# One 512-column product in place of two in the output and down-projections of a two-layer trunk

## The chip, the cores and the metric

One core of a Trainium2 chip runs the whole program in one launch. The metric is the device time of one execution in microseconds (us), the median of several executions. TensorE (PE in the profile) multiplies; VectorE (DVE) and ScalarE (ACT) do the elementwise work; the DMAs are issued from SyncE's queue (SP). All weights and activations lie in HBM as fp32.

## What is computed

The reference is a decoder trunk of two layers over 256 tokens of width 1024, cut here to what matters:

```python
for i in range(DEPTH):                      # 2 layers
    mod = sc @ w_ada[i] + b_ada[i]          # six rows of 1024: shift, scale, gate, twice
    sh_m, sc_m, g_m, sh_f, sc_f, g_f = jnp.split(mod, 6, axis=-1)
    h = modulate(x, norm_mix[i], sh_m, sc_m)
    y = moba_attention(h, ..., w_o[j], ...) if i % 2 == 0 else short_conv(h, ..., w_out[j])
    x = x + g_m[:, None, :] * y
    h = modulate(x, norm_ffn[i], sh_f, sc_f)
    x = x + g_f[:, None, :] * swiglu(h, w_gate_up[i], w_down[i])   # hidden width 2816
```

Attention has 8 heads of width 128, the convolution has width 3. The change is in the three kinds of products that end a sub-layer: `@ w_o` (attention's output), `@ w_out` (the convolution's output) and `@ w_down`, each followed by the gated addition to x.

## The kernel before

**Layout.** x is kept transposed in SBUF as `xT`: 8 column tiles (k = 0 to 7) of 128 features by 256 tokens. Activations that enter a product have the same layout. Weights are the stationary operand, 128 by 128; the 256 tokens stream past them.

**Precision.** Every fp32 operand is split in a high and a low part (fp32r): ACT makes the high part, DVE subtracts it for the low part. A product of two fp32 operands is three products, `mm3` (L246): high weights with the high activations (L248), high weights with the low activations (L249), low weights with the high activations (L250), summed in PSUM. Names ending in h and l are the parts: `wh_o`, `wl_o` for the weights, `ovh`, `ovl` for attention's output, `zvh`, `zvl` for the convolution's, `a0h`, `a0l` (layer 0) and `a1h`, `a1l` (layer 1) for the hidden activations of the channel mixer.

**Weights.** They come in pieces of 1 MB (256 output columns by 8 row tiles; the last piece of a down-projection has 6): a DMA (L88) into one of 5 buffers `wf`, then `prep` (L91) makes `wh` on ACT (L98) and `wl` on DVE (L99), each in two halves of 4 row tiles, into one of 3 buffers each. `get` (L240) prepares up to two pieces ahead. Between them pieces of `w_ada` come by the same five buffers (`wa`) and are summed on DVE into the shifts, scales and gates (`prod`, L109).

**The projections.** `out_proj` (L360) makes the 1024 output features as 4 column pairs j of two tiles o each. `op_o` and `op_co` have 8 row tiles to sum, `op_d` has 22. For `op_o` and `op_co` the pairs run in the groups [0, 1], [2], [3], for `op_d` each alone. Each (j, o) has a PSUM tile of one bank (4 in turn). After a group, at high priority, `residual` (L357) adds the gated sum to `xT` on DVE, one instruction of 128x256 for each (j, o), and `Norm.take` (L312) begins the next norm: squares on ACT (`sq_n`), their sum on DVE (`ss_n`), and the unnormalized next input in two parts (`a0h` on ACT, `a0l` on DVE; `zvh`, `zvl` before the convolution).

**The next sub-layer's start.** `raw_gemm` (L398) multiplies that unnormalized input for the first pieces before the norm is known (`raw_f`, `raw_m`: 96 products of 258 columns, the two extra columns carrying the shift). While it runs, the mean square goes over PE (`ms_n`), ACT (`sd_n`), DVE (`rs_n`), PE (`rr_n`) and ACT (`rrow_n`), and DVE and ACT make the normalized input (`t_f`, `f0h`, `f0l`; `m1h`, `m1l`) for the rest.

**Order.** A scheduler orders each engine's instructions from the program's order, its priorities and its own estimate of when things are ready. So instructions of `op_o` and of `raw_f` may stand between each other.

The stages in the profile: `op_o` until 130.4 us (its first group between attention's heads from 98 us), `raw_f` until 143.1, gate and up of layer 0 until 254, `op_d` of layer 0 until 318.4, `raw_m` until 331, the convolution's input until 388, `op_co` until 411, `raw_f` of layer 1 until 423.7, its gate and up until 533, its `op_d` until 592.7.

Of the kernel before, what the change touches and what calls it, by code (L numbers as in the profile page):

```python
# [8 lines left out]
F32 = mybir.dt.float32  # L9
# [6 lines left out]
P = 128  # L16
S = 256
# [16 lines left out]
def trunk_kernel(ctx: ExitStack, tc: tile.TileContext, x_t, cols_in, scale_in, shift_in, ada_in, qk_rows, kv_in, o_in,  # L34
# [106 lines left out]


    def room(tag, n, name, dtype=F32):
        size = {"al": KF * S + 16, "ah": KF * S, "zh": KD * (S + 32), "zl": KD * (S + 2)}.get(tag, KD * S)
        return act.tile([P, size], dtype, tag=tag, name=name)[:, 16 if tag == "al" else 0:][:, :n]

# [5 lines left out]

    room("al", 1, "first_al")
    xT = act.tile([P, KD, S], F32, name="xT")
    hs = new_pair("h", "m0", KD)
    room("ah", 1, "first_ah")
    x_tok = room("zh", 2 * D, "x_tok").rearrange("p (t d) -> p t d", d=D)
    for t in range(2):
# [87 lines left out]
    def mm3(ps, lhs, rhs, first, last):  # L246
        (ah, al), (bh, bl) = lhs, rhs
        nc.tensor.matmul(ps, ah, bh, start=first, stop=False, skip_group_check=True)  # L248
        nc.tensor.matmul(ps, ah, bl, start=False, stop=False, skip_group_check=True)  # L249
        nc.tensor.matmul(ps, al, bh, start=False, stop=last, skip_group_check=True)  # L250

    def feat_gemm(parts, xs, nk):
# [21 lines left out]

    RAW = KD * (S + 2)

    def wide_pair(name):
        flat = [room("z" + p, RAW, name + p, F32R) for p in "hl"]
        return (tuple(f[:, :KD * S].rearrange("p (k s) -> p k s", s=S) for f in flat),
                tuple(f.rearrange("p (k s) -> p k s", s=S + 2) for f in flat))  # L280

    def raw_in(pair):
        flat = [t.rearrange("p k s -> p (k s)") for t in pair]
        return tuple(f[:, KF * S - RAW:].rearrange("p (k s) -> p k s", s=S + 2) for f in flat)

# [71 lines left out]
    def residual(ps, l, gate, k):  # L357
        nc.vector.scalar_tensor_tensor(xT[:, k], ps, mcol(l, gate, k), xT[:, k], op0=ALU.mult, op1=ALU.add)

    def out_proj(keys, xs, l, gate, done, between={}):  # L360
        groups = [[0, 1], [2], [3]] if len(keys[0]) == 1 else [[j] for j in range(4)]
        for js in groups:
            pss = {(j, o): psum.tile([P, S], F32, tag="gemm", name=f"op_{keys[j][0][0][0]}_{l}_{j}_{o}", bufs=4)
                   for j in js for o in range(2)}
            base = 0
            total = sum(nk for _, nk in keys[0])
            for i, (_, nk) in enumerate(keys[0]):
                ws = {j: get(keys[j][i][0]) for j in js}
                tiles = [(j, o, k) for j in js for o in range(2) for k in range(nk)]
                if js[0] == 0:  # L370
# [12 lines left out]
            with tc.high_priority(400):  # L383
                for (j, o), ps in pss.items():
                    residual(ps, l, gate, 2 * j + o)
                    done(2 * j + o)

    def split(dst, k, src, name, psum_src=False):
        nc.scalar.activation(dst[0][:, k], src, AF.Copy)
        nc.vector.tensor_sub(dst[1][:, k], src, dst[0][:, k].bitcast(F32))  # L390
# [36 lines left out]
    def ffn(l, norm, av, done):  # L427
        for j in range(KF // 2):
# [6 lines left out]
            else:  # L435
# [102 lines left out]
    with tc.manual_schedule(engines={mybir.EngineType.PE, mybir.EngineType.DVE, mybir.EngineType.Activation}):  # L538
# [212 lines left out]

    av = new_pair("a", "a0", KF)
    n0 = Norm("n0", 0, SH_F, SC_F, raw_in(av))
    out_proj([[(("o", j), KD)] for j in range(4)], ov, 0, G_M, n0.take, between(6))
    zv, zraw = wide_pair("zv")
    n1 = Norm("n1", 1, SH_M, SC_M, zraw)
# [110 lines left out]
```

## Time and profile before

| | |
|---|---|
| time, median of 3 runs | 597.29 us (597.12 to 597.96) |
| the profiled execution's own time | 597.81 us |
| its span in the trace | 596.0 us |
| granted TensorE clock | 1.00 |
| DMA, share of the 16 engines' span | 69.9%, 156.04 MB |

Times within the trace count from the span's start. In rows of the trace the columns are: start, busy time, engine, line, operation, output <- inputs, shapes, count of merged records, and in square brackets the idle time before it with what ended it. A record of a product lasts longer than the spacing of the products' starts, since they are pipelined; costs are read from the spacing. A plain fp32 product (not fp32r) is recorded as two passes. PEld is PE's loading of the 128x128 weights, which overlaps the products.

### The profile page before, as it was taken

The page shows a single profiled execution, that of the slowest core. Times are in us where ns is not written, and L with a number is a line of the kernel's source. Part 1 is how long each engine was busy: PE and PEld are TensorE (multiplying, and loading weights), DVE is VectorE, ACT ScalarE, POOL GpSimd, SP SyncE. Part 2 cuts the span into 40 slices and gives each one's busy share as a digit, 9 for nine tenths or more (in the row PEclk, how much of TensorE's full clock was granted, in tenths as well). Part 3 has the DMA queues.
Part 4 walks back from the last instruction along what each step waited for, and adds up shares of the span by engine and source line. Part 5 has one row for each costly group of instructions (what it writes and reads, how often), then busy time and mean ns, then how long its engine had stood idle before and what let it go on. Part 6 is the DMA issues. An engine that isn't in the chain of part 4 may idle for free.

```text
span 596.0 us, 12024 instructions
## 1 busy us (share of the span) xinstructions
PE 587.8 (99%) x5036; PEld 579.0 (97%) x5036; DVE 454.5 (76%) x719; ACT 314.1 (53%) x526; POOL 1.1 (0%) x8
## 2 busy tenths in 40 slices
PE   7999999999999999999999999999999999999997
PEld 6899999999999999999999999999999999999997
DVE  4789898898988879877877998659987566564440
ACT  6457799596544544534444754437844554443330
POOL 0000000000000000000000000000000000000000
PEclk9999999999999999999999999999999999999999
DMA  8999988945897899777987477544486574655400
GB/s 323 392 373 411 361 332 300 369 162 180 329 388 296 303 358 356 268 279 276 330 317 292 148 293 278 207 142 184 170 323 249 206 283 164 252 186 190 165 19 18
DMA packets 25109, 156.04 MB, mean 262 GB/s; under 512 B 2784, under 2 KB 3168, under 8 KB 8928
## 3 DMA queue, kind: packets, MB, share of 16 engines
q1 hardware_dynamic: 25056, 155.28, 69.9%
q8 instruction: 39, 0.64, 0.4%
q14 instruction: 14, 0.11, 0.1%
HBM read 154.22 MB, written 1.05 MB: 261 GB/s over the span
## 4 chain that ended last, share of the span: by engine, by line
PE 89%; DVE 4%; DMA 3%; ACT 2%; issue 1%; SPq 0%; DVEq 0%; ACTq 0%
PE pu L250 7%; PE pu L249 7%; PE pu L248 7%; PE op_d L249 7%; PE op_d L248 7%; PE op_d L250 7%; PE pg L249 6%; PE pg L248 6%; PE pg L250 6%; PE op_o L248 1%; PE raw_f L248 1%; PE raw_f L249 1%; PE op_o L250 1%; PE op_co L250 1%; PE raw_f L250 1%; DMA wa<-in_ada_dram 1%
## 5 line engine op out<-in xcount | busy, mean ns | idle before, releaser
L109 DVE SCALAR_TENSOR_TENSOR prod<-wa,c_all 128x1024 f32<-128x1024 f32 x80 | 97.6, 1220 | 13.9 <-DMA wa<-in_ada_dram 13.0
L98 ACT ACTIVATE wh_d<-wf_d 128x1024 fp32r<-128x1024 f32 (+1 forms) x48 | 45.3, 981 | 67.2 <-issue 46.5
L99 DVE TENSOR_TENSOR wl_d<-wf_d,wh_d 128x1024 fp32r<-128x1024 f32 (+1 forms) x48 | 52.9, 1132 | 26.4 <-ACT wh_d L98 26.4
L98 ACT ACTIVATE wh_g<-wf_g 128x1024 fp32r<-128x1024 f32 x44 | 45.7, 1051 | 47.0 <-issue 47.0
L98 ACT ACTIVATE wh_u<-wf_u 128x1024 fp32r<-128x1024 f32 x44 | 44.5, 1051 | 48.4 <-issue 48.0
L99 DVE TENSOR_TENSOR wl_u<-wf_u,wh_u 128x1024 fp32r<-128x1024 f32 x44 | 52.2, 1219 | 16.7 <-ACT wh_u L98 16.5
L99 DVE TENSOR_TENSOR wl_g<-wf_g,wh_g 128x1024 fp32r<-128x1024 f32 x44 | 53.3, 1219 | 2.5 <-ACT wh_g L98 2.4
L249 PE MATMUL op_d<-a0l,wh_d 128*128 128x256 f32 x176 | 49.3, 280 | 0.0
L248 PE MATMUL op_d<-a0h,wh_d 128*128 128x256 f32 x176 | 49.1, 279 | 0.0
L250 PE MATMUL op_d<-a0h,wl_d 128*128 128x256 f32 x176 | 49.1, 279 | 0.0
L248 PE MATMUL op_d<-a1h,wh_d 128*128 128x256 f32 x176 | 48.6, 276 | 0.0
L249 PE MATMUL op_d<-a1l,wh_d 128*128 128x256 f32 x176 | 48.6, 276 | 0.0
L250 PE MATMUL op_d<-a1h,wl_d 128*128 128x256 f32 x176 | 48.6, 276 | 0.0
L249 PE MATMUL pg<-f0l,wh_g 128*128 128x256 f32 x160 | 44.8, 280 | 0.0
L249 PE MATMUL pu<-f0l,wh_u 128*128 128x256 f32 x160 | 44.8, 280 | 0.0
L248 PE MATMUL pg<-f0h,wh_g 128*128 128x256 f32 x160 | 44.7, 280 | 0.0
L250 PE MATMUL pg<-f0h,wl_g 128*128 128x256 f32 x160 | 44.6, 279 | 0.0
L248 PE MATMUL pu<-f0h,wh_u 128*128 128x256 f32 x160 | 44.6, 279 | 0.0
L250 PE MATMUL pu<-f0h,wl_u 128*128 128x256 f32 x160 | 44.6, 279 | 0.0
L248 PE MATMUL pg<-f1h,wh_g 128*128 128x256 f32 x160 | 44.2, 277 | 0.0
L249 PE MATMUL pg<-f1l,wh_g 128*128 128x256 f32 x160 | 44.2, 276 | 0.0
L250 PE MATMUL pg<-f1h,wl_g 128*128 128x256 f32 x160 | 44.2, 276 | 0.0
(296 smaller groups left out, 2024.8 us busy)
## 6 DMA issues: line engine op xcount, KB each, us to landing
wa<-in_ada_dram SPq DMA_DIRECT2D x40, 1024.0 KB, 5.3
wf_g<-in_gate_up_dram SPq DMA_DIRECT2D x22, 1024.0 KB, 4.9
wf_u<-in_gate_up_dram SPq DMA_DIRECT2D x22, 1024.0 KB, 4.9
wf_d<-in_down_dram SPq DMA_DIRECT2D x16, 1024.0 KB, 5.3
wf_d<-in_down_dram SPq DMA_DIRECT2D x8, 768.0 KB, 5.4
wa_sc<-in_scale_dram SPq DMA_DIRECT2D x8, 512.0 KB, 6.7
wa_sh<-in_shift_dram SPq DMA_DIRECT2D x8, 512.0 KB, 7.6
wf_qk<-in_qk_rows_dram SPq DMA_DIRECT2D x8, 512.0 KB, 6.5
```

The source lines that it names most:

```text
L98: nc.scalar.activation(wh[:, a:b], wf[:, a:b], AF.Copy)
L99: nc.vector.tensor_sub(wl[:, a:b], wf[:, a:b], wh[:, a:b].bitcast(F32))
L109: nc.vector.scalar_tensor_tensor(t, w, 1.0, c_all, op0=ALU.mult, op1=ALU.mult, accum_out=dst)
L248: nc.tensor.matmul(ps, ah, bh, start=first, stop=False, skip_group_check=True)
L249: nc.tensor.matmul(ps, ah, bl, start=False, stop=False, skip_group_check=True)
L250: nc.tensor.matmul(ps, al, bh, start=False, stop=last, skip_group_check=True)
```

## The change

For `op_o`, `op_co` and `op_d` the two parts of an activation tile now lie side by side in SBUF (256 high, then 256 low columns). The new `mm2` makes one product of the high weights with all 512 columns, into both halves of a PSUM bank, and one of the low weights with the 256 high columns, which adds to the second half. `residual` then runs twice, for either half. Only the last tile, (j, o) = (3, 1), keeps `mm3` and one residual. Of 480 (tile, row tile) pairs 420 use `mm2` (56 each in `op_o` and `op_co`, 154 in each `op_d`): 420 PE products fewer and 28 residuals more. `ovh`/`ovl` become `ov`, `zvh`/`zvl` `zv`, `a0h`/`a0l` `a0`.

```diff
+    RAW_L = RAW + 112
+    RAW_A = S + P
     def room(tag, n, name, dtype=F32):
-        size = {"al": KF * S + 16, "ah": KF * S, "zh": KD * (S + 32), "zl": KD * (S + 2)}.get(tag, KD * S)
+        size = {"a": 2 * KF * S + 16, "z": RAW_L + RAW}.get(tag, KD * S)
...
+    def mm2(ps, lhs, rhs, first, last):
+
+        ah, al = lhs
+        nc.tensor.matmul(ps, ah, rhs, start=first, stop=False, skip_group_check=True)
+        nc.tensor.matmul(ps[:, 1], al, rhs[:, 0], start=False, stop=last, skip_group_check=True)
...
+    def side_by_side(flat):
+        both = flat.rearrange("p (k a s) -> p k a s", a=2, s=S)
+        return (both[:, :, 0], both[:, :, 1]), both
...
     def out_proj(keys, xs, l, gate, done, between={}):
...
-            pss = {(j, o): psum.tile([P, S], F32, tag="gemm", name=f"op_{keys[j][0][0][0]}_{l}_{j}_{o}", bufs=4)
+            pss = {(j, o): psum.tile([P, 2, S], F32, tag="gemm", name=f"op_{keys[j][0][0][0]}_{l}_{j}_{o}", bufs=4)
...
-                    mm3(pss[j, o], (wh[:, k, cs], wl[:, k, cs]), (xs[0][:, base + k], xs[1][:, base + k]),
-                        base + k == 0, base + k == total - 1)
+
+                    prod, ps = (mm3, pss[j, o][:, 0]) if (j, o) == (3, 1) else (mm2, pss[j, o])
+                    prod(ps, (wh[:, k, cs], wl[:, k, cs]), xs[:, base + k], base + k == 0, base + k == total - 1)
...
-                    residual(ps, l, gate, 2 * j + o)
+                    for i in range(1 if (j, o) == (3, 1) else 2):
+                        residual(ps[:, i], l, gate, 2 * j + o)
                     done(2 * j + o)
```

The scheduler orders anew around it. Below, in a name such as `op_o_0_3_1_1740`, the digits are layer, j, o and a running number; `wl_o_3` is the low part of `op_o`'s fourth piece, `wl_u_0_0` that of the first up piece of layer 0.

VectorE where `op_o`'s first group ends, before:

```order
L358 SCALAR_TENSOR_TENSOR xT_102<-op_o_0_1_1_1480,mod_99,xT_102 128x256
L99 TENSOR_TENSOR wl_o_3_1517<-wf_o_3_1514,wh_o_3_1516 128x1024
L329 SCALAR_TENSOR_TENSOR a0l_1476<-xT_102,mod_99,a0h_1475 128x256
L99 TENSOR_TENSOR wl_g_0_0_1672<-wf_g_0_0_1669,wh_g_0_0_1671 128x1024
L319 TENSOR_TENSOR ss_n0_1_1651<-sq_n0_0_1644,sq_n0_1_1649 128x256
L329 SCALAR_TENSOR_TENSOR a0l_1476<-xT_102,mod_99,a0h_1475 128x256 x3
L322 TENSOR_TENSOR ss_n0_1_1651<-ss_n0_1_1651,sq_n0_2_1656 128x256
L358 SCALAR_TENSOR_TENSOR xT_102<-op_o_0_2_0_1667,mod_99,xT_102 128x256
L322 TENSOR_TENSOR ss_n0_1_1651<-ss_n0_1_1651,sq_n0_3_1662 128x256
L358 SCALAR_TENSOR_TENSOR xT_102<-op_o_0_2_1_1668,mod_99,xT_102 128x256
L99 TENSOR_TENSOR wl_o_3_1517<-wf_o_3_1514,wh_o_3_1516 128x1024
L99 TENSOR_TENSOR wl_u_0_0_1744<-wf_u_0_0_1741,wh_u_0_0_1743 128x1024
```

and now:

```order
L345 SCALAR_TENSOR_TENSOR a0_1471<-xT_102,mod_99,a0_1471 128x256
L335 TENSOR_TENSOR ss_n0_1_1616<-sq_n0_0_1608,sq_n0_1_1614 128x256
L345 SCALAR_TENSOR_TENSOR a0_1471<-xT_102,mod_99,a0_1471 128x256 x2
L338 TENSOR_TENSOR ss_n0_1_1616<-ss_n0_1_1616,sq_n0_2_1622 128x256
L345 SCALAR_TENSOR_TENSOR a0_1471<-xT_102,mod_99,a0_1471 128x256
L338 TENSOR_TENSOR ss_n0_1_1616<-ss_n0_1_1616,sq_n0_3_1629 128x256
L374 SCALAR_TENSOR_TENSOR xT_102<-op_o_0_2_0_1634,mod_99,xT_102 128x256
L99 TENSOR_TENSOR wl_u_0_0_1697<-wf_u_0_0_1694,wh_u_0_0_1696 128x1024
L374 SCALAR_TENSOR_TENSOR xT_102<-op_o_0_2_0_1634,mod_99,xT_102 128x256
L374 SCALAR_TENSOR_TENSOR xT_102<-op_o_0_2_1_1635,mod_99,xT_102 128x256
L99 TENSOR_TENSOR wl_o_3_1512<-wf_o_3_1509,wh_o_3_1511 128x1024
L338 TENSOR_TENSOR ss_n0_1_1616<-ss_n0_1_1616,sq_n0_4_1678 128x256
```

Ahead of these rows there now stand 8 residuals in place of 4, then the first halves of `wl_o_3` and `wl_g_0_0`. The second half of `wl_o_3` stood ahead of the first half of `wl_u_0_0` and behind two residuals of pair 2; now it stands behind that half and behind three residuals of pair 2.

PE at `op_o`'s last pair, before; the row on `wl_o_3` that ends it is the first that reads the second half:

```order
L249 MATMUL op_o_0_3_0_1739<-ovl_743,wh_o_3_1516 128x256
L248 MATMUL op_o_0_3_1_1740<-ovh_742,wh_o_3_1516 128x256
L249 MATMUL op_o_0_3_1_1740<-ovl_743,wh_o_3_1516 128x256
L250 MATMUL op_o_0_3_1_1740<-ovh_742,wl_o_3_1517 128x256
L248 MATMUL op_o_0_3_1_1740<-ovh_742,wh_o_3_1516 128x256
L249 MATMUL op_o_0_3_1_1740<-ovl_743,wh_o_3_1516 128x256
L250 MATMUL op_o_0_3_1_1740<-ovh_742,wl_o_3_1517 128x256
L248 MATMUL op_o_0_3_1_1740<-ovh_742,wh_o_3_1516 128x256
L250 MATMUL op_o_0_3_0_1739<-ovh_742,wl_o_3_1517 128x256
```

and, from the same place, a part of what now stands ahead of that row:

```order
L253 MATMUL op_o_0_3_1_1693<-ov_739,wh_o_3_1511 128x256
L254 MATMUL op_o_0_3_1_1693<-ov_739,wh_o_3_1511 128x256
L253 MATMUL raw_f0_10_1757<-a0_1471,wh_u_0_0_1696 128x258
L254 MATMUL raw_f0_10_1757<-a0_1471,wh_u_0_0_1696 128x258
L255 MATMUL raw_f0_10_1757<-a0_1471,wl_u_0_0_1697 128x258
L253 MATMUL raw_f0_00_1755<-a0_1471,wh_g_0_0_1638 128x258
L254 MATMUL raw_f0_00_1755<-a0_1471,wh_g_0_0_1638 128x258
L255 MATMUL raw_f0_00_1755<-a0_1471,wl_g_0_0_1639 128x258
L253 MATMUL raw_f0_11_1758<-a0_1471,wh_u_0_0_1696 128x258
```

Between the last product on the first half of `wh_o_3` of tile (3, 0) and that row stand 14 products of tile (3, 1) and 16 of `raw_f` now, where 7 of tile (3, 1) stood. In `op_co` the scheduler does the like: ahead of the first product on `wl_co_3` stand 2 products of layer 1's `raw_f`, and ahead of the first on its second half 20 more.

VectorE behind layer 0's `op_d`, before (`wa_1_3_1` is the `w_ada` piece that `prod_1_3_1` sums):

```order
L99 TENSOR_TENSOR wl_cb_0_4014<-wf_cb_0_4011,wh_cb_0_4013 128x1024
L347 RECIPROCAL rs_n1_4063<-sd_n1_4062 128x2
L109 SCALAR_TENSOR_TENSOR prod_1_3_1_0_4324,mod_99<-wa_1_3_1_4322,c_all_100 128x1024
L109 SCALAR_TENSOR_TENSOR prod_1_3_1_1_4326,mod_99<-wa_1_3_1_4322,c_all_100 128x1024
L295 SCALAR_TENSOR_TENSOR t_m1_0_4097<-xT_102,mod_99,rrow_n1_4090 128x256
```

and now:

```order
L99 TENSOR_TENSOR wl_cb_0_3812<-wf_cb_0_3809,wh_cb_0_3811 128x1024
L109 SCALAR_TENSOR_TENSOR prod_1_3_1_0_4122,mod_99<-wa_1_3_1_4120,c_all_100 128x1024
L363 RECIPROCAL rs_n1_3861<-sd_n1_3860 128x2
L109 SCALAR_TENSOR_TENSOR prod_1_3_1_1_4124,mod_99<-wa_1_3_1_4120,c_all_100 128x1024
L311 SCALAR_TENSOR_TENSOR t_m1_0_3895<-xT_102,mod_99,rrow_n1_3888 128x256
```

The reciprocal of the norm now stands behind a sum that waits for a DMA. Ahead of these rows both halves of `wl_cg_0` were moved in front of the two sums of `wa_1_3_0`.

More of the change, by code (lines that the diff above doesn't have):

```diff
@@ L139, in first_rows @@
         return wf
+    RAW = KD * (S + 2)
+    RAW_L = RAW + 112
+    RAW_A = S + P
     def room(tag, n, name, dtype=F32):
-        size = {"al": KF * S + 16, "ah": KF * S, "zh": KD * (S + 32), "zl": KD * (S + 2)}.get(tag, KD * S)
-        return act.tile([P, size], dtype, tag=tag, name=name)[:, 16 if tag == "al" else 0:][:, :n]
+        size = {"a": 2 * KF * S + 16, "z": RAW_L + RAW}.get(tag, KD * S)
+        return act.tile([P, size], dtype, tag=tag, name=name)[:, 16 if tag == "a" else 0:][:, :n]
     def pair_rows(flat):
@@ L151, in new_pair @@
         return tuple(pair_rows(room(tag + p, nk * S, name + p, F32R)) for p in "hl")
-    room("al", 1, "first_al")
+    room("a", 1, "first_a")
     xT = act.tile([P, KD, S], F32, name="xT")
     hs = new_pair("h", "m0", KD)
-    room("ah", 1, "first_ah")
-    x_tok = room("zh", 2 * D, "x_tok").rearrange("p (t d) -> p t d", d=D)
+    first = room("z", RAW_L + RAW, "first_z")
+    x_tok = first[:, :2 * D].rearrange("p (t d) -> p t d", d=D)
     for t in range(2):
@@ L246, in mm3 @@
     def mm3(ps, lhs, rhs, first, last):
-        (ah, al), (bh, bl) = lhs, rhs
+        ah, al = lhs
+        bh, bl = rhs if isinstance(rhs, tuple) else (rhs[:, 0], rhs[:, 1])
         nc.tensor.matmul(ps, ah, bh, start=first, stop=False, skip_group_check=True)
@@ L270, in tok_gemm, with long_pair @@
                         k == 0 and t == 0, k == nk - 1)
-    RAW = KD * (S + 2)
+    def side_by_side(flat):
+        both = flat.rearrange("p (k a s) -> p k a s", a=2, s=S)
+        return (both[:, :, 0], both[:, :, 1]), both
     def wide_pair(name):
[L278 to L284, printed above, removed]
+        f = room("z", RAW_L + RAW, name, F32R)
+        return side_by_side(f[:, :2 * KD * S]), tuple(f[:, i:i + RAW].rearrange("p (k s) -> p k s", s=S + 2)
+                                                      for i in (0, RAW_L))
+    def long_pair(name):
+        f = room("a", 2 * KF * S, name, F32R)
+        n = KD * RAW_A
+        return side_by_side(f), tuple(f[:, 2 * KF * S - i * n:][:, :n].rearrange("p (k s) -> p k s", s=RAW_A)[:, :, :S + 2]
+                                      for i in (2, 1))
     def rstd_rows(r, name):
@@ L442, in ffn @@
                 nc.vector.tensor_mul(a, s, pu)
-            split(av, slice(2 * j, 2 * j + 2), a, f"{l}_{j}")
-        out_proj([[(("d", l, j, i), n) for i, n in enumerate((8, 8, 6))] for j in range(4)], av, l, G_F, done)
+            split(av[0], slice(2 * j, 2 * j + 2), a, f"{l}_{j}")
+        out_proj([[(("d", l, j, i), n) for i, n in enumerate((8, 8, 6))] for j in range(4)], av[1], l, G_F, done)
     def mod_sums(w, name):
@@ L555, in trunk_kernel @@
         keep_warm(6)
-        sq = room("zl", RAW, "sq0")
+        sq = first[:, RAW_L:][:, :2 * D]
         ssq = const.tile([P, 2], F32, name="ssq0")
@@ L613, in trunk_kernel @@
                 ops = ops_n
-    qT = room("ah", 2 * H * S, "qkT").rearrange("p (a h s) -> p a h s", a=2, h=H)
-    vp = room("al", 2 * D + H * 3 * P, "vp")
+    attn = room("a", 2 * H * S + 2 * D + H * 3 * P, "attn")
+    qT = attn[:, :2 * H * S].rearrange("p (a h s) -> p a h s", a=2, h=H)
+    vp = attn[:, 2 * H * S:]
     v_sb = vp[:, :2 * D].rearrange("p (t d) -> p t d", d=D)
@@ L708, in turn_probs @@
         nc.scalar.activation(probs[:, h], pt[:, :3 * P], AF.Copy)
-    ov, _ = wide_pair("ov")
+    (ov, ov_rows), _ = wide_pair("ov")
     def mix_values(h):
@@ L750, in trunk_kernel @@
         nc.scalar.activation(v_sb[:, :, j * CW:(j + 1) * CW], pv, AF.Copy)
[L752 to L755, printed above, removed]
+    av, av_raw = long_pair("a0")
+    n0 = Norm("n0", 0, SH_F, SC_F, av_raw)
+    out_proj([[(("o", j), KD)] for j in range(4)], ov_rows, 0, G_M, n0.take, between(6))
+    (zv, zv_rows), zraw = wide_pair("zv")
     n1 = Norm("n1", 1, SH_M, SC_M, zraw)
@@ L793, in trunk_kernel @@
             split(zv, slice(2 * j, 2 * j + 2), z, f"z{j}")
-    av = new_pair("a", "a1", KF)
-    n2 = Norm("n2", 1, SH_F, SC_F, raw_in(av))
-    out_proj([[(("co", j), KD)] for j in range(4)], zv, 1, G_M, n2.take)
+    av, av_raw = long_pair("a1")
+    n2 = Norm("n2", 1, SH_F, SC_F, av_raw)
+    out_proj([[(("co", j), KD)] for j in range(4)], zv_rows, 1, G_M, n2.take)
     def store(k):
```

1 line of the change is left out of this document (added).

## The prediction

> **What bounds the kernel now.** The page's busy times and its chain come first.
>
> ```profile
> PE 587.8 (99%) x5036; PEld 579.0 (97%) x5036; DVE 454.5 (76%) x719; ACT 314.1 (53%) x526; POOL 1.1 (0%) x8
> PE 89%; DVE 4%; DMA 3%; ACT 2%; issue 1%; SPq 0%; DVEq 0%; ACTq 0%
> PE op_o L248 <- ACT ovh L389: 0.5, 1, 0.5
> ```
>
> PE works all the time, and the view of PE's waits holds little in the stages that change: 0.5 us in `op_o` is the largest. So the time is the number of PE products times their spacing. The windows view gives the spacing: stage by stage from gate and up of layer 0, its `op_d`, `op_co`, gate and up of layer 1, its `op_d`; the last row is `op_o`'s pairs 2 and 3.
>
> ```profile
> 144.00:248.00 104.00, 104.00 (x886) 1.00 0.83 315
> 256.00:316.00 60.00, 60.00 (x512) 1.00 0.78 284
> 386.00:410.00 24.00, 24.00 (x206) 1.00 0.30 105
> 425.00:532.00 107.00, 107.00 (x947) 1.00 0.64 233
> 536.00:592.00 56.00, 56.00 (x496) 1.00 0.29 99
> 119.50:126.90 7.40, 7.40 (x68) 1.00 0.16 66
> ```
>
> A window counts some 2.4 products too many, since records of 0.28 us overlap at its edge. 104.0/883.6 and 60.0/509.6 give 117.7 ns, 24.0/203.6 gives 117.9, but 107.0/944.6 gives 113.3, 56.0/493.6 gives 113.5 and 7.4/65.6 gives 112.8. The same instruction has **two paces, 117.8 and 113.3 ns**, at a granted clock of 1.00 in all six rows. Each holds for a whole stage.
>
> What sets the pace? These are one-column products of the norm, then `raw_f` (first and last of 19 in a row), and plain fp32 passes with the product behind them.
>
> ```profile
> 133.67 0.36 PE L341 MATMUL ms_n<-inv_d,ss_n 128*128 128x1 f32 x2
> 133.89 0.36 PE L342 MATMUL ms_n<-inv_d,sq_n 128*128 128x1 f32 x2
> 134.12 0.36 PE L248 MATMUL raw_f<-a0h,wh_g 128*128 128x258 f32 x1
> ...
> 131.04 0.28 PE L250 MATMUL raw_f<-a0h,wl_g 128*128 128x258 f32 x1
> 133.19 0.28 PE L250 MATMUL raw_f<-a0h,wl_u 128*128 128x258 f32 x1
> ...
> 110.71 0.59 PE L715 MATMUL po<-vp 128*128 128x256 f32 x2
> 111.14 0.38 PE L716 MATMUL po<-vp 128*128 128x128 f32 x2
> ```
>
> Two passes of a single column start 0.22 us apart, so one with next to nothing to stream still costs 112 ns: that is what a weight load costs (PEld is 97% busy). The plain passes of 256 columns take 0.43/2 = 215 ns each: a pass whose streaming is longer than a load hides the load. Products of 256 fp32r columns sit just above the load, so I read them as held by the load and its hand-over, not by their columns.
>
> **The gain.** An `mm2` tile is one 512-column product and one of 256 where three of 256 stood. No row shows a 512-column product. From below it costs one load (112), from above two narrow ones (235.6 or 226.6). The lower end I exclude: 18 steps of `raw_f` from 131.04 to 133.19 are 119.4 ns each, so two more columns are felt, and 256 columns lie close under the load. I take **215 ns**, the plain pass, as the nearest row: it has twice the streaming of an fp32r pass if 256 fp32r columns take some 107. The upper end stays as a rival. Then a tile costs 215 + 117.8 = 332.8 in place of 353.4 in the slow pace (20.6 saved), 328.3 in place of 339.9 in the fast one (11.6 saved):
>
> - layer 0's `op_d`: 154 x 20.6 = 3.2 us
> - layer 1's `op_d`: 154 x 11.6 = 1.8
> - `op_co`: 56 x 20.6 = 1.2
> - `op_o`: 32 tiles of the first group x 20.6 and 24 x 11.6 = 0.9
>
> Together **7.1 us**. The lone narrow product behind the wide one has its load hidden under 215 ns; the next load still starts with it, so I leave it at the old pace.
>
> The Trainium skill, page "TensorE: Matmul & The Clock Gate", section "Back-to-back issue gap", speaks against this: an isolated warm product costs N/2.4 + 2.5 ns, which is 215.8 for 512 columns and 109.2 for 256. The trace agrees at 215 and not at 117.8 or 113.3. By the rule alone a tile would save 2.6 ns, 1.1 us in all. The same page's section on LDWEIGHTS estimates 128/1.2 = 107 ns a load, near the 112 above; that is why I do not follow the gap rule.
>
> **What is lost: VectorE's queue.** 28 more residuals cost nothing where DVE has slack, as in `op_d`. But at the ends of `op_o` and `op_co` DVE has no idle time:
>
> ```profile
> 117.56 0.42 DVE L390 TENSOR_TENSOR ovl<-po,ovh 128x256 fp32r<-128x256 f32 x1 [0.81 <-ACT ovh L389]
> 117.57 0.74 PE L248 MATMUL op_o<-ovh,wh_o 128*128 128x256 f32 x4 [0.47 <-ACT ovh L389]
> 118.59 1.66 DVE L358 SCALAR_TENSOR_TENSOR xT<-op_o,mod,xT 128x256 f32<-128x256 f32 x4 [0.61 <-PE op_o L250]
> 120.17 1.21 DVE L99 TENSOR_TENSOR wl_o<-wf_o,wh_o 128x1024 fp32r<-128x1024 f32 x1
> 125.49 0.48 DVE L358 SCALAR_TENSOR_TENSOR xT<-op_o,mod,xT 128x256 f32<-128x256 f32 x1
> 125.89 1.21 DVE L99 TENSOR_TENSOR wl_o<-wf_o,wh_o 128x1024 fp32r<-128x1024 f32 x1
> 127.02 1.22 DVE L99 TENSOR_TENSOR wl_u<-wf_u,wh_u 128x1024 fp32r<-128x1024 f32 x1
> 127.15 0.38 PE L250 MATMUL op_o<-ovh,wl_o 128*128 128x256 f32 x1
> 118.59:136.30 17.71, 17.71 (x32) 1.00 0.53 192
> ```
>
> *Last head, -0.4.* Before, four high products ran from 117.57 while `ovl` was made. A 512-column product needs both parts, so PE waits for `ovl`, 0.42 us.
>
> *End of `op_o`, -0.7.* The second half of `wl_o` was ready at 127.10 and taken at 127.15: just in time. It now stands behind five more residuals (0.40 apart in the row of four: 2.0) and `wl_u`'s first half (1.13 from 125.89 to 127.02): 3.1 us further down. With the first residual at about 118.1 (28 tiles of the first group have gained 0.6) it is ready at 118.1 + 8.5 + 3.1 = 129.7. PE, from 118.8: 16 tiles of pair 2, 5.3 us; four and a half of tile (3, 0), 1.5; 14 products of tile (3, 1), 1.6; so it is at `raw_f` at 127.25, and wants `wl_u`'s first half at 127.5, ready at 127.75: 0.25. Then 14 more products of 0.12 bring it to 129.45 and a wait of 0.25. So the moved `raw_f` products are the cover; without them the wait would be 16 x 0.12 = 1.9 us longer. The sum of squares, behind the same queue, ends near 135.6, where PE wants it at 135.4: 0.2.
>
> *End of `op_co`, -0.6.* The same queue, 17 us without idle time. By the same steps the first half of `wl_co` comes 0.4 late behind seven residuals, `wl_u` and the second half 0.1 each; 22 products of `raw_f` fill the rest (2.6 us without them).
>
> ```profile
> 398.98 1.66 DVE L358 SCALAR_TENSOR_TENSOR xT<-op_co,mod,xT 128x256 f32<-128x256 f32 x4 [6.26 <-PE op_co L250]
> 406.24 1.22 DVE L99 TENSOR_TENSOR wl_co<-wf_co,wh_co 128x1024 fp32r<-128x1024 f32 x1
> 398.98:416.50 17.52, 17.52 (x31) 1.00 0.38 138
> ```
>
> *Behind layer 0's `op_d`, -0.3.* `rs_n` now waits for the DMA of `wa_1_3_1`.
>
> ```profile
> 318.45 0.33 SPq L88 DMA_DIRECT2D wa<-in_ada_dram  x1
> 323.94 0.17 DVE L347 RECIPROCAL rs_n<-sd_n 128x2 f32<-128x2 f32 x1 [0.35 <-ACT sd_n L346]
> 325.04 0.38 PE L290 MATMUL rr_n<-ident,rs_n 128*128 128x128 f32 x2
> 326.02 1.23 DVE L109 SCALAR_TENSOR_TENSOR prod<-wa,c_all 128x1024 f32<-128x1024 f32 x1 [1.92 <-DMA wa<-in_ada_dram]
> ```
>
> PE comes to `rr_n` about 3.2 us earlier, at 321.9. The transfer took 7.6 us from its issue; it is issued when `wl_cu` frees its buffer, which I put at 313.7 since `wl_cg` no longer waits behind `wa`. It lands between 319.6 and 321.3, the sum takes 1.2: `rs_n` at 320.8 to 322.5, a wait of 0 to 0.8; taken 0.3. If the issue is no earlier than now, it is 326.02 + 1.2 - 321.9, over 5 us; the DMA's share of 0.78 in `op_d` speaks against that.
>
> *Starts of gate and up, -0.3.* `f0h`, `f0l` come later by the 2 us that DVE lags, but 5 us of slack before becomes 2 to 3. Products of `pu` stand between those of `pg` there.
>
> The stores are untouched: the last tile keeps one residual.
>
> Sum: 597.81 - 7.1 + 2.3 = 593.0 for the profiled execution; it lies 0.5 above the median, so **592.6 us**.
>
> **Rivals.**
>
> 1. *The pace of layer 1's channel mixer falls back to 117.8* (0.17). Nothing in the change asks for it, but the rows show the same instruction at either pace from stage to stage, and I see no cause in the code, only that the pace holds until PE is interrupted; every interruption moves. 960 products x 4.5 ns and 176 tiles at 4.5 to 13.5 ns: 5.3 us, giving 597.9.
> 2. *The same lottery the other way* (0.17): layer 0's gate and up, or the convolution, run at 113.3. 960 x 4.5 + 1.0 = 5.3, giving 587.3; the convolution's 480 give 590.4.
> 3. *A fixed cost on every product* (0.12): the excess over streaming (117.8 - 107.5 = 10.3, or 5.8) stays on the wide one. For it: `raw_f`'s two columns are felt. Against: the plain pass of 256 columns shows no excess over twice 107.5. Gain 154 x 10.3 + 154 x 5.8 + 56 x 10.3 + 0.5 = 3.5 us, giving 596.1. The gap rule of the Trainium skill's page above would be the extreme of this, 1.1 us of gain: 598.5.
> 4. *Slower: the wide product costs two narrow ones*, 235.6 or 226.6 (0.05), in all 420 tiles. No gain, only the 2.3 us of waits: 599.6. It decides from 420 tiles saving less than 2.3 us, 5.5 ns a tile, a wide product above 230 ns in the slow pace. No row excludes it; the plain pass speaks against.
> 5. *The queue is longer than reckoned* (0.06): `raw_f`'s moved products wait too, and 1.9 + 2.6 us come back: 597.1.
>
> That the change does not do what it says is no rival here: 420 PE rows fewer stand in the built program.
>
> **How the numbers follow.** The forecast has 0.43. 0.2%, about what a measurement of this kernel can tell from no change, is 1.2 us: faster is below 596.1, slower above 598.5. Faster: forecast (0.41), rival 2 (0.17), half of 3 and a part of 5: 0.66. Same: the other half of 3, most of 1, the rest of 5: 0.19. Slower: rival 4, the worse part of 1 with more waits, the forecast's tail: 0.15. The range goes from 588.0 (rival 2 in part) to 598.5 (rivals 1 and 3): the long `wa` wait and rival 4 are left out.
>
> **What would show it.** Windows inside both `op_d`: a tile at 333 and 328 ns is right, 343 is rival 3, 353 rival 4. Gate and up windows give the paces. The row of PE's `L261` on `wl_o` behind `raw_f` shows 0.25 us of wait, the one on `wl_co` 0.1; 2 us is rival 5. `rr_n` behind `raw_m` shows 0 to 0.8. The forecast is wrong if the wide product's spacing is not near 215, or if a pace changes in a stage that the change does not touch.

## The result, and the profile after

| | before | after |
|---|---|---|
| median, us (range) | 597.2 (596.8 to 598.0) | 605.6 (604.9 to 606.4) |
| ratio, 95% interval | | 1.014 (1.0122 to 1.0158) |
| span of the profiled execution | 596.0 | 603.9 |

The change makes the kernel 1.4% slower; 592.6 was forecast. The page of the kernel after has these busy times and this chain:

```profile
PE 594.4 (98%) x4616; PEld 566.5 (94%) x4616; DVE 466.8 (77%) x747; ACT 314.4 (52%) x526; POOL 1.1 (0%) x8
...
PE 93%; ACT 3%; DMA 2%; DVE 1%; issue 0%; SPq 0%; ACTq 0%
```

420 products fewer, and PE is busy 6.6 us longer. The view of its waits (us in total, times, longest) has three rows on the output projections, and none on the down-projections:

```profile
PE op_o L260 <- DVE ov L408: 0.9, 1, 0.9
...
PE op_co L260 <- DVE xT L374: 0.4, 1, 0.4
PE op_o L260 <- DVE xT L374: 0.4, 1, 0.4
```

They are small. The windows view of the kernel after, gate and up of layer 0 and of layer 1 (in parentheses the number of products):

```profile
150.00:248.00 98.00, 98.00 (x834) 1.00 0.87 322
432.00:538.00 106.00, 106.00 (x902) 1.00 0.64 233
```

Less the 2.4 products that a window counts too many, layer 0 keeps its pace with 98.0/831.6 = 117.8 ns, but layer 1 has lost its own: 106.0/899.6 = 117.8 where 113.3 stood.

The timeline of the kernel after gives the price of an `mm2` tile: below are the first, second and last of 86 wide products in a row in layer 0's `op_d`, then of 87 in layer 1's. The first column is the start.

```profile
261.87 0.40 PE L260 MATMUL op_d<-a,wh_d 128*128 128x512 f32 x1
262.22 0.40 PE L260 MATMUL op_d<-a,wh_d 128*128 128x512 f32 x1
...
291.90 0.40 PE L260 MATMUL op_d<-a,wh_d 128*128 128x512 f32 x1
...
544.77 0.40 PE L260 MATMUL op_d<-a,wh_d 128*128 128x512 f32 x1
545.12 0.39 PE L260 MATMUL op_d<-a,wh_d 128*128 128x512 f32 x1
...
574.78 0.39 PE L260 MATMUL op_d<-a,wh_d 128*128 128x512 f32 x1
```

30.03/85 = **353.3 ns** and 30.01/86 = **349.0 ns** for a wide and a narrow product together. Three narrow ones took 353.4 and 339.9 at these places. So the new tile gains nothing in layer 0 and loses 9 ns in layer 1.

Stage by stage, from the starts of the first product of each stage in the two traces (us); gate and up and the convolution begin with the two one-column `settle` products:

| stage | before | after | change | forecast |
|---|---|---|---|---|
| up to the first `op_o` product | 104.24 | 104.81 | +0.6 | 0 |
| `op_o` and `raw_f` of layer 0 | 38.78 | 39.67 | +0.9 | +0.2 |
| gate and up of layer 0 | 113.22 | 113.51 | +0.3 | +0.2 |
| `op_d` of layer 0 | 62.19 | 62.19 | 0 | -3.2 |
| `raw_m` | 12.59 | 12.64 | 0 | +0.3 |
| convolution | 57.52 | 56.68 | -0.8 | 0 |
| `op_co` and `raw_f` of layer 1 | 35.17 | 35.79 | +0.6 | -0.6 |
| gate and up of layer 1 | 108.95 | 113.56 | +4.6 | +0.1 |
| `op_d` of layer 1 | 59.73 | 61.44 | +1.7 | -1.8 |
| sum | | | +7.9 | -4.8 |

Two questions remain: why a wide product gains nothing, and why layer 1's gate and up, where the change edits nothing, became slower. The second is the larger.

### The profile page after: what moved, and what is told of

It reads as the page before. It is cut to its first block, busy times and chain, and to the rows that moved or that the text cites. A ratio compares the mean times of both kernels' runs of the same rounds, so it can differ in the third digit from the quotient of the medians.

```text
span 603.9 us, 11201 instructions
## 1 busy us (share of the span) xinstructions
PE 594.4 (98%) x4616; PEld 566.5 (94%) x4616; DVE 466.8 (77%) x747; ACT 314.4 (52%) x526; POOL 1.1 (0%) x8
## 4 chain that ended last, share of the span: by engine, by line
PE 93%; ACT 3%; DMA 2%; DVE 1%; issue 0%; SPq 0%; ACTq 0%
PE op_d L260 12%; PE pu L255 7%; PE pu L253 7%; PE pu L254 7%; PE pg L253 6%; PE op_d L261 6%; PE pg L255 6%; PE pg L254 6%; PE op_o L260 2%; PE op_co L260 2%; PE pb L253 1%; PE pb L254 1%; PE raw_f L253 1%; PE pb L255 1%; PE raw_f L254 1%; PE raw_f L255 1%
## 5 line engine op out<-in xcount | busy, mean ns | idle before, releaser
L260 PE MATMUL op_d<-a,wh_d 128*128 128x512 f32 x308 | 108.5, 395 | 0.0
L261 PE MATMUL op_d<-a,wl_d 128*128 128x256 f32 x308 | 86.6, 281 | 0.0
L260 PEld LDWEIGHTS op_d<-a,wh_d 128*128 128x128 f32 x308 | 57.9, 188 | 13.5
L261 PEld LDWEIGHTS op_d<-a,wl_d 128*128 128x128 f32 x308 | 57.8, 188 | 0.0
L255 PE MATMUL pu<-f1h,wl_u 128*128 128x256 f32 x160 | 44.8, 280 | 0.0
L253 PE MATMUL pu<-f1h,wh_u 128*128 128x256 f32 x160 | 44.6, 279 | 0.0
```

What stands on the lines that cost most here:

```text
L260: nc.tensor.matmul(ps, ah, rhs, start=first, stop=False, skip_group_check=True)
L261: nc.tensor.matmul(ps[:, 1], al, rhs[:, 0], start=False, stop=last, skip_group_check=True)
```

## The experiments

Times stand against 597.1 to 597.6 for the kernel before, measured on the same chip each time. "Pitch" is the time from one product's start to the next.

**1. What a product of n columns costs.** The changed kernel; in layer 0 the gate and up tiles run at other widths, from their second row tile on, and so do the wide products of `op_d`. Parts of the sums are left out or added there. One execution was taken.

```diff
...
+                cols = (0, 256, 240, 224, 192, 160, 128, 64, 512, 384, 256)[j] if l == 0 else S
-                feat_gemm([(pg, get(("g", l, j)))], hs, KD)
-                feat_gemm([(pu, get(("u", l, j)))], hs, KD)
+                feat_gemm([(pg, get(("g", l, j)))], hs, KD, cols)
+                feat_gemm([(pu, get(("u", l, j)))], hs, KD, cols)
...
```

> The changed kernel with other numbers of columns in layer 0, which leaves out or adds parts of the sums there: gate and up pieces j = 1 to 10 stream 256, 240, 224, 192, 160, 128, 64, 512, 384, 256 columns in every product but those of the first row tile, and op_d's wide products of column pairs 0 to 3 stream 512, 448, 384, 320 columns. Theory C (columns: every fp32r column costs 0.44 to 0.46 ns in any product, and the weight load lies under it): spacing 0.46 x columns, so 230 to 236 ns at 512 and 170 to 177 at 384, down to a floor near 112 at 240 columns and below; op_d tiles 353, 324, 294, 265 ns. Theory S (a product above 256 columns is run as two, each with its own fixed part): 236 at 512, but 112 + 118 = 230 at 384 too; op_d tiles with 448, 384 and 320 columns all near 345 to 353. Theory F (a fixed part of about 10 ns on each product besides 0.42 ns a column): 223 at 512, 170 at 384; op_d tiles at 512 near 341.

Its timeline shows the first and last of 36 products of 512 columns, of 37 of 384, of 38 of 240 and of 38 of 160:

```profile
274.83 0.39 PE L255 MATMUL pu<-f0h,wl_u 128*128 128x512 f32 x1
...
282.83 0.39 PE L254 MATMUL pu<-f0l,wh_u 128*128 128x512 f32 x1
284.69 0.34 PE L254 MATMUL pg<-f0l,wh_g 128*128 128x384 f32 x1
...
290.93 0.34 PE L254 MATMUL pg<-f0l,wh_g 128*128 128x384 f32 x1
...
156.75 0.27 PE L254 MATMUL pg<-f0l,wh_g 128*128 128x240 f32 x1
...
160.88 0.27 PE L255 MATMUL pg<-f0h,wl_g 128*128 128x240 f32 x1
...
204.33 0.28 PE L254 MATMUL pg<-f0l,wh_g 128*128 128x160 f32 x1
...
208.46 0.27 PE L255 MATMUL pg<-f0h,wl_g 128*128 128x160 f32 x1
```

8.00/35 = 228.6 ns, 6.24/36 = 173.3, 4.13/37 = 111.6 and again 111.6. From 512 to 384 columns the pitch falls by 55.3 (0.43 ns a column), from 384 to 256 by another 55.5, to 117.8. So a product costs **0.434 ns a column and 6.7 ns beside**, down to a floor of 111.6 that 240 and 160 columns share. 256 columns stand above the floor: they are held by their columns. A wide product of 229 ns replaces two narrow ones of 235.6, so at most 6.6 ns a tile can be saved, not 20.6. In `op_d`, where the widths alternate, a tile whose wide product had 448, 384 or 320 columns took 319, 293 and 263 ns; the law gives 319, 291 and 263.

The Trainium skill, page "TensorE: Matmul & The Clock Gate", section "Back-to-back issue gap", has N/2.4 + 2.5 ns for an isolated warm product, 215.8 at 512 columns. The trace does not agree: 229, with a slope of 0.434 in place of 0.417 ns a column.

**2. One tiny product more.** The kernel before, where `settle` issues three one-column bf16 products in place of two, at three places (one execution).

```diff
-        for i in range(2):
+        for i in range(3):
             nc.tensor.matmul(ps[:, i:i + 1], one_b.to_broadcast([P, P]), one_b, start=True, stop=True, skip_group_check=True)
```

> The kernel before with three one-column bf16 products in place of two between raw_f or raw_m and what follows; nothing else is touched. Theory L (the pace of a stage is set anew, as if by lot, where PE is interrupted): at least one of the three stages behind them (gate and up of layer 0, the convolution, gate and up of layer 1, before at 117.8, 117.8 and 113.3 ns) changes its pace, and the time moves by 2 to 10 us either way. Theory A (the pace follows from where the operands lie in SBUF, which the change moved): all three stay as before, time 597 us within 1.

603.7 us: three more products, 25 ns each, cost 6.5 us. The windows view of this run has layer 1's gate and up at 107.0/908.6 = 117.8 ns; before, the same window held 947 products.

```profile
425.00:532.00 107.00, 107.00 (x911) 1.00 0.63 229
```

**3. The layout alone, and the down-projections alone.** The changed kernel with `mm3` and one residual in every tile; and with `mm2` in the down-projections only. The edit of the first:

```diff
-                    prod, ps = (mm3, pss[j, o][:, 0]) if (j, o) == (3, 1) else (mm2, pss[j, o])
+                    prod, ps = mm3, pss[j, o][:, 0]
...
-                    for i in range(1 if (j, o) == (3, 1) else 2):
+                    for i in range(1):
```

> The change's layout of the activations alone, with mm3 and one residual in every tile. Theory A: gate and up of layer 1 run at 117.8 ns as in the changed kernel, so 597 + 4.6 = 602 us or more. Theory L: the pace of layer 1's gate and up may be either; where it is 113.3 the time is 597 us within 1. Theory C says that op_d of layer 0 takes 62.2 us as in both kernels.

> mm2 and two residuals in op_d alone; op_o and op_co with mm3 and one residual. The VectorE queue's theory: the 0.95 us that the changed kernel has lost by the end of raw_f of layer 0 and the 0.6 us by that of layer 1 are gone (within 0.3). Theory C: op_d of layer 0 at 62.2 us, op_d of layer 1 at 60 to 61.6 by its pace. Theory L: gate and up of layer 1 at either pace; Theory A: at 117.8.

604.1 us (ratio 1.0123, 1.0099 to 1.0147) and 604.1 (1.0116, 1.0095 to 1.0136). With no wide product in it, the kernel with the layout alone is slower by 6.9 us, of the change's 8.4. Its window on layer 1's gate and up reads like that of experiment 2, and so do all its other stages:

```profile
425.00:532.00 107.00, 107.00 (x911) 1.00 0.62 228
```

In the second of the two the tiles of the down-projections took 349 ns in layer 0 and 353 in layer 1, the other way round than in the changed kernel. Its output projections, back at `mm3`, together with `raw_f` took 39.05 and 35.13 us, 0.6 and 0.7 less than in the changed kernel: but for 0.3 in layer 0, what those stages lose comes with `mm2` and its residuals there.

**4. Interruptions of many kinds.** The kernel before, with an interruption ahead of each of the 40 full gate and up tiles: one of 20 kinds of short bf16 products, then in a second run one fp32r product of 20 widths (one execution each). The edit of the first:

```diff
...
+        for i in range(n):
+            nc.tensor.matmul(ps[:, i * cols:(i + 1) * cols], one_b.to_broadcast([P, P]), one_b.to_broadcast([P, cols]),
+                             start=True, stop=True, skip_group_check=True)
...
```

> The kernel before, with a short interruption ahead of every full gate and up tile of both channel mixers (40 places): 1 to 12 one-column bf16 products, or 2 to 4 of 4 to 96 columns, the same 20 kinds in layer 0 and, in reverse order, in layer 1. Theory L (a stage keeps, until the next interruption, one of two paces that the interruption left it in, whatever runs in the stage): each tile of 48 products runs wholly at 113.3 or wholly at 117.8 ns, the pace changes only at interruptions, and both occur in both layers; in the settled part of the tile nothing else is seen. If the kind of interruption decides, one kind gives the same pace in both layers; if it is a matter of the moment, one kind gives different ones, with the fast one in perhaps 1 to 4 of 20. Theory A (the pace follows where the operands lie in SBUF, or the layer): all 20 tiles of layer 0 at 117.8 and all 20 of layer 1 at 113.3, as before. The pauses themselves cost about 0.1 to 0.4 us each, some 8 us, so the time is 597 to 612 us and is not what is read.

> The kernel before, with one more fp32r product of 16 to 252 columns (20 widths, in reverse order in layer 1) into an unused bank ahead of every full gate and up tile of both channel mixers. The earlier run with bf16 interruptions found one fast tile in 40. Theory L with a pace that is a matter of the moment: again each tile is wholly at 113.3 or wholly at 117.8 ns, with few fast ones (0 to 4 of 40) and none of the widths fast in both layers. If the phase between weight loads and products that an interruption leaves decides it, and a width sets that phase, then some widths (those a few columns off 256 among them) give the fast pace in both layers, and a kernel could be steered into it. The added products cost about 0.11 us each, 4.5 us in all: 601 to 609 us.

612.3 and 610.8 us. Of 80 tiles one was fast, 79 slow. The fast one (the first and last of 42 products) and the next tile (41) in the timeline of the first run:

```profile
440.00 0.28 PE L248 MATMUL pg<-f1h,wh_g 128*128 128x256 f32 x1
...
444.65 0.28 PE L250 MATMUL pg<-f1h,wl_g 128*128 128x256 f32 x1
...
445.76 0.28 PE L249 MATMUL pu<-f1l,wh_u 128*128 128x256 f32 x1
...
450.47 0.28 PE L250 MATMUL pu<-f1h,wl_u 128*128 128x256 f32 x1
```

4.65/41 = 113.4 ns, 4.71/40 = 117.8. In these 80 tiles the pace changes only at an interruption, here between two neighbouring tiles of one stage with the same activations. The same kind of interruption (three products of 64 columns) gave 117.8 in layer 0. So neither the layer nor the place of the operands fixes it; what does was still unknown.

One in 80 is not the rate everywhere. In the attention's projections of the kernel before (12 to 104 us), where other products and short waits interrupt PE again and again, there are 22 stretches of at least nine 256-column fp32r products with no pitch above 121 ns; 14 of them began at the fast pace. There the pace also fell three times with no product between, each time where `pq` gives way to `pk`. The timeline of the kernel before has the first and last of 24 `pq` and of 11 `pk` products behind them:

```profile
35.23 0.28 PE L248 MATMUL pq<-m0h,wh_qk 128*128 128x256 f32 x1
...
37.84 0.28 PE L250 MATMUL pq<-m0h,wl_qk 128*128 128x256 f32 x1
37.95 0.28 PE L248 MATMUL pk<-wh_qk,m0h 128*128 128x256 f32 x1
...
39.13 0.28 PE L249 MATMUL pk<-wl_qk,m0h 128*128 128x256 f32 x1
```

2.61/23 = 113.5 ns, then 1.18/10 = 118. So what was said of interruptions holds for the mixers.

**5. The same interruptions, repeated.** Only the three interruptions that led to the fast tile, in three kernels: before, after, and the second kernel of experiment 6 below.

```diff
...
+    PAUSES = {("g", 1): (1, 64), ("u", 1): (4, 32), ("g", 2): (3, 64)}
...
```

> The kernel before with only the three interruptions of layer 1 that ended in the fast tile of the earlier run: one product of 64 columns ahead of the first full gate tile, four of 32 ahead of the first up tile, three of 64 ahead of the second gate tile, and none after them. If the sequence of products since the channel mixer's start decides the pace, the first two tiles run at 117.8 and all that follows in the mixer and the down-projection, 864 + 528 products, at 113.3 ns: against a run that is slow throughout (603.7 us) that is 1392 x 4.5 = 6.3 us less and 0.5 us more for the pauses, 598 us. If the moment decides (the phase in which the earlier stages happened to leave TensorE), the mixer runs at 117.8 in all tiles: 604 us. The first interruption takes away the fast entry that the kernel before had at this place in either case.

> The changed kernel with the same three interruptions. If the sequence since the mixer's start decides: the mixer's tiles from the third on at 113.3 ns, 864 x 4.5 = 3.9 us less, and the last down-projection's pairs (349.2 ns) at 340 to 346 ns, 0.5 to 1.4 us less: 605.6 + 0.5 - 4.9 = 601 us. If the moment decides: 117.8 ns throughout and 606 us.

> The kernel with 512-column products grouped by width in the first three pairs of the down-projections (602.7 us), with the same three interruptions. If the sequence decides: 3.9 us less in the mixer and up to 1.5 us in the last down-projection, 0.5 us for the pauses: about 598 us. If the moment decides: 603 us.

598.1 us (1.0015, 1.0004 to 1.0026), 606.6 and 602.2. In the kernel before, the fast pace came back at the same place and held to the end; its window behind the third interruption gives 95.0/837.6 = 113.4 ns:

```profile
435.00:530.00 95.00, 95.00 (x840) 1.00 0.66 243
```

In the other two the mixer stayed at 117.8. They had come to it otherwise, as the pitch of the first product behind the first interruption shows: 204 ns in both kernels with the fast tile, 203 and 200 in these; that this is the reason was not tested. So in the kernel before it is no chance of the moment: the same sequence gave the same pace a second time.

**6. Wide products in a row.** The changed kernel with the 512-column products of each piece of the down-projections' weights first and its 256-column ones behind them; and the same in the first three pairs of the down-projections only, with `mm3` everywhere else.

```diff
+                    if total > KD and prod is mm2:
+                        nc.tensor.matmul(ps, wh[:, k, cs], xs[:, base + k], start=base + k == 0, stop=False,
+                                         skip_group_check=True)
+                        continue
...
+                for j, o, k in tiles if total > KD else ():
...
+                        nc.tensor.matmul(pss[j, o][:, 1], wl[:, k, o * P:(o + 1) * P], xs[:, base + k, 0], start=False,
+                                         stop=base + k == total - 1, skip_group_check=True)
```

> The changed kernel, with the products of one down chunk in the down-projections put in another order: all 512-column products of the chunk first, then its 256-column ones. Theory F (each product costs 6.7 ns beside 0.434 ns a column at the slow pace: 229.0, 173.3 and 117.8 ns for 512, 384 and 256 columns where products of one width follow each other; a mix of widths costs 2 to 6 ns more a pair): one wide and one narrow product cost 229.0 + 117.8 = 346.8 ns instead of the 353.3 and 349.2 that the alternating order took, so op_d0 and op_d1 lose 154 x 6.5 = 1.0 and 154 x 2.4 = 0.4 us against the changed kernel, and the kernel comes to 604.2. Theory C (columns alone, no fixed part; the pair costs 353.3 in any order): no change, 605.6. If a pair in the grouped order takes 340, the pace has fallen to the fast one: 603.5 or less.

> The part of the change that can gain, alone: the changed kernel's layout, 512-column products only in the first three pairs of the two down-projections, there grouped by width, and three narrow products with one residual everywhere else. Theory F with paces left alone (all stages at 117.8): against the run of the layout alone (604.08 us), 132 pairs in each down-projection take 346.6 instead of 353.3 ns, 0.88 us each, and the boundaries after the output projections and the tail are as there: 604.08 - 1.8 = 602.3 us. Theory C (no gain in a wide product): 604.1. If some stage falls into the fast pace, it shows in the trace as 113.3 ns a product, and takes off 2 to 7 us more: below 600.5. In no case does it beat the kernel before without that.

604.9 us (1.0121, 1.0095 to 1.0147) and 602.7 (1.008, 1.0055 to 1.0105): 0.8 us less than the change, and 1.4 less than the layout alone (1.8 expected). These intervals overlap with those of the kernels compared; the traces are clearer, with `op_d` at 61.2 and 61.1 us in the second run where the layout alone has 62.2 and 62.1. In the first run's timeline two pieces of pair 0 and one of pair 2:

```profile
262.96 3.83 PE L399 MATMUL op_d<-a,wh_d 128*128 128x512 f32 x16
266.63 2.05 PE L406 MATMUL op_d<-a,wl_d 128*128 128x256 f32 x16
268.51 2.92 PE L399 MATMUL op_d<-a,wh_d 128*128 128x512 f32 x12
...
291.57 1.98 PE L406 MATMUL op_d<-a,wl_d 128*128 128x256 f32 x16
293.38 2.91 PE L399 MATMUL op_d<-a,wh_d 128*128 128x512 f32 x12
```

Wide: (266.63 - 262.96)/16 = 229.4 ns. Narrow behind them: 1.88/16 = 117.5. So a pair costs 346.9 when the widths are kept apart, as the law of experiment 1 says, and the alternation of the change costs 2 to 6 ns more: that is where the 6.6 ns went. The group at 291.57 took 1.81/16 = 113.1: a fast one, in the middle of a slow stage. That gave the next idea. Behind the first two to four, wide products in a row do not take 229 each but about 226, 229 and 232 in turn, and the groups behind them differ by where this cycle of three stopped.

**7. Steering.** Four dummy wide products into an unused bank at two places of the kernel before: ahead of the second full tile of layer 0's mixer and ahead of the third one of the convolution.

```diff
+    def steer(name, w, x, n):
+        ps = ps_misc("steer_" + name)
+        for i in range(n):
+            nc.tensor.matmul(ps, w[:, 0, :P], x[:, 0:2].rearrange("p k s -> p (k s)"), start=True, stop=True,
+                             skip_group_check=True)
...
+                if (l, j) == (0, 1):
+                    steer("f0", uj[0], hs[0], 4)
...
```

> The kernel before with four more 512-column products into an unused bank at two places: ahead of the second full tile of layer 0's channel mixer, and ahead of the third full tile of the convolution. In the grouped runs a sequence of 512-column products repeated 226, 229, 232 ns, and all 18 to 20 groups of narrow products behind it ran at 113.3 ns where the last wide one had taken 231 or 232, and at 117.8 where it had taken 226 or 229. Theory P (the pace is set by the phase of this cycle of three, and is kept): at each of the two places the narrow products behind run at 113.3 if the fourth wide one takes 231 or 232, else at 117.8, which happens by the phase that the stage began in, one of three; a hit in layer 0 takes 912 + 528 products x 4.5 = 6.5 us off and costs 0.9, a hit in the convolution 400 + 192 products x 4.5 = 2.7 us off for 0.9. Both hit: 589.9 us; layer 0 alone: 592.6; neither: 599.1, in each case with layer 1 fast as in the kernel before; 6.5 us more where it is lost there. Theory L (a matter of the moment): neither, and the last wide product's time tells nothing.

The windows view of this run: layer 0's gate and up, its `op_d`, the convolution, layer 1's gate and up, its `op_d`.

```profile
150.50:252.00 101.50, 101.50 (x898) 1.00 0.90 337
254.00:312.00 58.00, 58.00 (x514) 1.00 0.80 299
339.00:380.00 41.00, 41.00 (x364) 1.00 0.75 280
418.00:524.00 106.00, 106.00 (x938) 1.00 0.64 234
527.00:584.00 57.00, 57.00 (x506) 1.00 0.30 104
```

101.5/895.6 = 113.3, 58.0/511.6 = 113.4, 41.0/361.6 = 113.4, and layer 1 fast as before: all five. The traced execution took 590.8 us. Over ten executions the median is 595.5 us, **0.9956 (0.9928 to 0.9984)** of the kernel before, but they spread from 590.8 to 598.2; what the others lost was not traced.

**8. Steering the changed kernel.** The same four products at three places of the changed kernel and of the second kernel of experiment 6, the grouped one: ahead of the second full up tile of both mixers and of the third full tile of the convolution.

> The changed kernel with four more 512-column products into an unused bank ahead of the third full up tile of both channel mixers and ahead of the third full tile of the convolution. Theory P (phase): a stage whose fourth wide product takes 231 or 232 ns goes on at 113.3 ns a product, whatever the layout; one hit in a mixer is worth about 816 x 4.5 = 3.7 us less 0.9, in the convolution 400 x 4.5 = 1.8 less 0.9; all three hit: 605.6 - 9.2 + 2.8 = 599 us; one or two of three hit: 601 to 605. The mixed pairs of the down-projections stay at 349 to 354 ns. Theory A (the layout, or what runs ahead, keeps the mixer slow): all stages at 117.8 and 608.4 us, whatever the last wide product took.

> The kernel with 512-column products grouped by width in the first three pairs of the down-projections (602.7 us), with the same twelve added products. Theory P: 602.7 - 9.2 + 2.8 = 596 us where all three hit, and each stage at 113.3 exactly where its fourth wide product took 231 or 232 ns; theory A: 605.5 us. Against the kernel before with four such products at two places (595.5 us, 590.8 in its fastest execution) it should not be faster, since in the fast pace a wide and a narrow product (229 + 113) take no less than three narrow ones (340).

605.1 us (1.0135, 1.0103 to 1.0167) and 594.4 (0.9969, 0.9945 to 0.9994). In the changed kernel's run the timeline shows the dummy products of layer 0 and of layer 1, each with the product behind, and the windows view the tiles behind them:

```profile
161.77 1.08 PE L419 MATMUL steer_f<-f0h,wh_u 128*128 128x512 f32 x4
162.69 0.28 PE L253 MATMUL pu<-f0h,wh_u 128*128 128x256 f32 x1
...
442.80 1.09 PE L419 MATMUL steer_f<-f1h,wh_u 128*128 128x512 f32 x4
443.73 0.28 PE L253 MATMUL pu<-f1h,wh_u 128*128 128x256 f32 x1
```

```profile
163.50:255.00 91.50, 91.50 (x779) 1.00 0.89 334
346.00:385.00 39.00, 39.00 (x345) 1.00 0.73 278
444.50:534.00 89.50, 89.50 (x792) 1.00 0.64 236
```

In layer 0 the four took 0.92 us (229, 232, 226, 229) and the mixer went on at 91.5/776.6 = 117.8. In layer 1 they took 0.93 (233, 236, 229, 232), and it went on at 89.5/789.6 = 113.3; so did the convolution, with the same four pitches. The changed kernel's layout does not forbid the fast pace. Its down-projections do: behind the fast mixer of layer 1 the alternating tiles took 353 ns from the second on. In the grouped kernel all three places were hit; it comes out level with experiment 7, not better.

Over all seven runs with rows of at least four wide products, narrow ones followed such a row 88 times. Behind a last wide product of 231 or 232 ns all 38 groups were fast; behind one of 225 to 230 all 50 were slow.

## Why the prediction was wrong

**What bounds the kernel: right.** PE is busy 98% of the time and the sum of pitches is the time. The two paces of 117.8 and 113.3 ns were read correctly, and that in the mixers a pace holds until PE is interrupted was shown (experiments 4 and 5); between `pq` and `pk` it changed without that.

**"Products of 256 fp32r columns sit just above the load, so I read them as held by the load": wrong.** This is the step that failed first. The floor of 112 ns was right (111.6), but 256 columns are above it, held by their own columns at 0.434 ns and 6.7 beside. The wide product was priced at 215 ns from a plain fp32 pass; it takes 229 in a row of its kind and 230 to 234 in the change's alternation. A tile then saves 0 in place of 20.6 in the slow pace and loses 9 in place of gaining 11.6 in the fast one. The whole gain of 7.1 us was absent: 0 in `op_d` of layer 0, and 154 x 9 = 1.4 us lost in layer 1, with 0.3 more for the last tile's 22 steps, which fell from 340 to 353. Rival 3 had the fixed cost right in kind and near in size (6.7 against 10.3); rival 4, the wide product as dear as two narrow ones, is what the alternation came to. "No row excludes it" was said, and it still got 0.05. The argument against rival 3, that the plain pass shows no excess over twice 107.5, was circular: 107.5 is half of that pass's 215.

**The pace of layer 1's mixer: priced right, its chance wrong.** Rival 1 had 960 products x 4.5 ns = 4.3 us, and the stage lost 4.6 (with one wait of 0.3 in its first tiles). It was given 0.17 with a lottery the other way at 0.17 as its equal. But in the mixers the fast pace is rare: one of 80 interruptions gave it. A fast mixer whose interruptions move is more likely to fall back than a slow one to become fast; the attention's projections show that the odds differ from stage to stage. Which of the moved products cost layer 1 its pace was not found: one more tiny product did the same in experiment 2. The range ended at 598.5 since rivals 1 and 4 were only weighed apart. Both came at once: the forecast's 592.6, without its gain of 7.1 and with the 5.3 of rival 1, is 605.0, and 605.6 was measured.

**The waits: the sum near, the places not.** 2.3 us were forecast for the five terms; the stages concerned show 0.9 + 0.3 + 0 + 0.6 = 1.8, of which 0.3 is `op_o`'s 67 fast products that became slow. *Last head, -0.4*: exact, 0.9 us on `ov` in place of 0.5 on `ovh`. *Ends of `op_o` and `op_co`*: the waits for `wl_o`, `wl_u` and `wl_co` did not show; in their place PE waited once in each, 0.4 us, for a residual on `xT` to free a bank. The cause named (28 more residuals in DVE's queue) fits; with `mm3` back in these two projections the loss was gone, but for those 0.3 (experiment 3). *`raw_m`, -0.3*: 0. *Starts of gate and up, -0.3*: 0.3 in layer 0 and 0.3 in layer 1, where it is within the 4.6.

**Not foreseen:** the convolution gained 0.8 us, since two stalls of PE that the kernel before had among its first products, 0.25 and 0.59 us, are gone; they are gone in experiment 2 too, so the change is not needed for it. The start of `op_o` moved by 0.6; in the other runs with the new layout the first product started between 103.71 and 104.74, so this is put down to the execution, which was not tested.

## What to carry to other kernels

Price a wider product from a row of its own kind, or from the slope of two widths: merging two products saves only the fixed part of one (6.6 ns here), and no load that was hidden already. Before a change to a PE-bound kernel, look whether some stages run faster than others with the same instruction; such a pace can be lost by an edit ahead of it as small as one tiny product, so it belongs in the forecast as a likely loss. To judge the edit itself, compare stages at the same pace.

## What the runs showed of the hardware

- A stream of fp32r products can be in one of two lasting rhythms, 113.3 or 117.8 ns at 256 columns, at a granted clock of 1.00. The fast one held for up to 1486 products in a row. In the mixers, interruptions led into it once in 80 times; in the attention's projections 14 of 22 stretches began with it.
- A row of 512-column products settles to 226, 229 and 232 ns in turn, and the place in that cycle where it ends tells the rhythm of the narrow products behind it (38 of 38 fast, 50 of 50 slow). Four dummy products steered into the fast one at seven of eight places; what in the chip keeps the cycle is open.
- 512- and 256-column products in alternation cost 349 or 353 ns a pair, 2 to 6 more than the two kinds in rows of their own, and did not stay in the fast rhythm.
- In layer 0's gate and up of experiment 1 the granted clock fell to 0.50 four times, each time at or behind a wait of PE for weights of 3.2 to 3.8 us. Three times, with products of 224 and 192 columns behind it, it was back after 3.4 us. The fourth time, ahead of the tiles of 128 and 64 columns, it stayed at 0.50 for 47.8 us with a product every 213 ns, and came back 2.5 us into the row of 512 columns. That the waits took it down and the few columns kept it down fits this; neither was tried apart.
